# ReLU and mean over rows: input tiles of 8 rows in six buffers in place of 16 rows in three

## The chip, the cores and the metric

The kernel runs on one core of a Trainium2 chip. The metric is the device time of one execution in microseconds (us); lower is better. The time before is 164.88 us, the median of three runs (164.74 to 164.88).

## The reference

```python
batch, seq, dim = 32, 512, 1024
x = np.random.randn(batch, seq, dim).astype(np.float32)

relu_x = np.maximum(x, 0)
return np.mean(relu_x, axis=-1).astype(np.float32)
```

The input has 32 x 512 = 16,384 rows of 1,024 float32 values, 67.1 MB. For each row the kernel clips at zero and takes the mean: 16,384 results, 64 KB.

## The kernel before

The 16,384 rows are laid over 128 partitions, J = 128 consecutive rows on each (512 KB of contiguous input a partition). A tile `xt` holds NB = 16 rows of every partition: 128 partitions x 64 KB, 8.4 MB, and BUFS = 3 such buffers exist. The program is written out in full; there is no loop on the chip.

**Loads.** All loads are issued by SP (SyncE), in program order. Seven full tiles come with one transfer each (L79). A load waits until its buffer has been computed. The eighth tile comes in pieces: `row_pieces` halves what is left of the tile, so 8, 4, 2 and 1 rows (L86), and the last row comes as a half and two quarters (`col_pieces`, L90). That makes 14 loads.

**Compute.** `rows` (L62) gives even rows to ACT (ScalarE, L15) and odd rows to DVE (VectorE, L20). Each clips one row of 1,024 values in place and sums it into one column of `sum_a` or `sum_v`; in the trace each such call shows as two instructions, the work and the reading of the accumulator.

**Scaling.** `finish(lo, hi)` multiplies the sums by 1/1024 into `res`, odd columns on DVE (L73), even columns on ACT (L74). It runs twice: `finish(0, j0)` for all columns of the full tiles, placed ahead of the first piece of the last tile, and `finish(j0, j0 + lo)` behind the pieces but the last.

**End.** The last two rows are cut between ACT and DVE and put together by three small DVE instructions (L106, L111, L116), and one store of 64 KB (L120) writes `res`.

DMA transfers run on sixteen DMA engines. Each partition's share of a load is one contiguous run, so each engine gets eight data packets and one semaphore packet of a load; a load counts as landed when all sixteen semaphore packets have arrived. The trace has a record of each packet and each semaphore update.

Of the kernel before, what the change touches and what calls it, by code (L numbers as in the profile page):

```python
# [1 line left out]

# [4 lines left out]

F32 = mybir.dt.float32
ALU = mybir.AluOpType
RELU = mybir.ActivationFunctionType.Relu  # L10


def act_row(nc, src, acc):

    nc.scalar.activation(out=src, in_=src, func=RELU, accum_out=acc)  # L15


def dve_row(nc, src, acc):

    nc.vector.tensor_scalar(  # L20
        out=src, in0=src, scalar1=0.0, scalar2=None,
        op0=ALU.max, op1=ALU.add, accum_out=acc,
    )


@with_exitstack
def kernel(
    ctx: ExitStack,
    tc: tile.TileContext,
    x: bass.AP,  # L30
    out: bass.AP,
):
    nc = tc.nc
    P = nc.NUM_PARTITIONS
    xf = x.flatten_outer_dims()
    R, D = xf.shape
    assert R % P == 0
    J = R // P
    inv = 1.0 / D
    xr = xf.rearrange("(p j) d -> p j d", p=P, j=J)  # L40
    outr = out.flatten().rearrange("(p j) -> p j", p=P, j=J)

    NB = 16
    BUFS = 3
    full = J // NB - 1

    row_pieces = []
    left = NB
    while left > 1:
        row_pieces.append(left // 2)  # L50
        left -= left // 2
    col_pieces = [D // 2, D // 4, D // 4]

    in_pool = ctx.enter_context(tc.tile_pool(name="in", bufs=BUFS))
    res_pool = ctx.enter_context(tc.tile_pool(name="res", bufs=1))
    sum_a = res_pool.tile([P, J], F32)
    sum_v = res_pool.tile([P, J], F32)
    res = res_pool.tile([P, J], F32)
    part_a = res_pool.tile([P, 2], F32)
    part_v = res_pool.tile([P, 4], F32)  # L60

    def rows(xt, lo, n, j0):  # L62

        for k in range(lo, lo + n):
            j = j0 + k
            if j % 2:
                dve_row(nc, xt[:, k, :], sum_v[:, j:j + 1])
            else:
                act_row(nc, xt[:, k, :], sum_a[:, j:j + 1])

    def finish(lo, hi):

        nc.vector.tensor_scalar_mul(out=res[:, lo + 1:hi:2], in0=sum_v[:, lo + 1:hi:2], scalar1=inv)  # L73
        nc.scalar.mul(out=res[:, lo:hi:2], in_=sum_a[:, lo:hi:2], mul=inv)  # L74

    for t in range(full):
        j0 = t * NB
        xt = in_pool.tile([P, NB, D], F32, name="xt")
        nc.sync.dma_start(out=xt, in_=xr[:, j0:j0 + NB, :])  # L79
        rows(xt, 0, NB, j0)  # L80

    j0 = full * NB
    xt = in_pool.tile([P, NB, D], F32, name="xt")
    lo = 0
    for n in row_pieces:
        nc.sync.dma_start(out=xt[:, lo:lo + n, :], in_=xr[:, j0 + lo:j0 + lo + n, :])  # L86
        lo += n
    c = 0
    for w in col_pieces:
        nc.sync.dma_start(out=xt[:, lo, c:c + w], in_=xr[:, j0 + lo, c:c + w])  # L90
        c += w

    finish(0, j0)
    lo = 0
    for n in row_pieces[:-1]:
        rows(xt, lo, n, j0)
        lo += n
    finish(j0, j0 + lo)


    last = xt[:, NB - 1, :]
    act_row(nc, xt[:, lo, :D // 2], part_a[:, 0:1])
    dve_row(nc, xt[:, lo, D // 2:], part_v[:, 0:1])
    act_row(nc, last[:, :D // 4], part_a[:, 1:2])
    dve_row(nc, last[:, D // 4:D // 2], part_v[:, 1:2])
    nc.vector.tensor_scalar(  # L106
        out=res[:, J - 2:J - 1], in0=part_a[:, 0:1], scalar1=part_v[:, 0:1], scalar2=inv,
        op0=ALU.add, op1=ALU.mult,
    )
    dve_row(nc, last[:, D // 2:3 * D // 4], part_v[:, 2:3])  # L110
    nc.vector.tensor_scalar(  # L111
        out=part_v[:, 1:2], in0=part_v[:, 1:2], scalar1=part_a[:, 1:2], scalar2=part_v[:, 2:3],
        op0=ALU.add, op1=ALU.add,
    )
    dve_row(nc, last[:, 3 * D // 4:], part_v[:, 3:4])
    nc.vector.tensor_scalar(  # L116
        out=res[:, J - 1:J], in0=part_v[:, 3:4], scalar1=part_v[:, 1:2], scalar2=inv,
        op0=ALU.add, op1=ALU.mult,
    )
    nc.sync.dma_start(out=outr, in_=res)  # L120


# [1 line left out]
_INS = ['x']  # L124
_OUTS = [((32, 512), 'float32')]


# [23 lines left out]
```

## Time and profile before

| | |
|---|---|
| median of three runs | 164.88 us |
| the profiled execution | 164.88 us |
| its span in the profile | 163.1 us |
| DVE busy | 75.4 us (46%) |
| ACT busy | 69.4 us (43%) |
| DMA, load and store queue | 96.0% of 16 engines' span |
| bytes moved, mean rate | 67.19 MB, 412 GB/s |
| loads from HBM, stores | 14, 1 |

The span is what the profiler shows of the program on the core; the profiled execution's own time is longer by what lies around it. Busy shares are means over the whole span. "A <- B" behind an instruction names what ended the idle time ahead of it. SPq is the queue from which SP issues transfers, and its lines tell what an issue waited for. A line number is that of the kernel's source, so all rows on DVE stand under L20 and all rows on ACT under L15.

### The profile page before, as it was taken

To read this page: it belongs to the slowest core of one execution; us is meant where nothing else is said; L and a number is where in the kernel's file an instruction comes from. 1 tells how busy PE (TensorE), PEld (TensorE's weight loads), DVE (VectorE), ACT (ScalarE), POOL (GpSimd) and SP (SyncE) were. 2 spreads that over 40 slices of the span, in tenths; PEclk is the share of its full clock that TensorE was granted. 3 is DMA by queue.
4 is the path that set the end of the run, shared out by engine and by line. 5 is a ranking of instruction groups with operands and counts; after the bars stand their busy time and mean duration, and the time that the engine had idled before them with its cause. 6 is when DMAs were issued, how large, how long until landed. Compare 5 with 4: busy or idle time off the path is not lost.

```text
span 163.1 us, 351 instructions
## 1 busy us (share of the span) xinstructions
DVE 75.4 (46%) x139; ACT 69.4 (43%) x133; POOL 0.2 (0%) x4
## 2 busy tenths in 40 slices
DVE  0000039900596008940099202990059700799993
ACT  3000039700594008920099002980059500797890
POOL 0000000000000000000000000000000000000000
DMA  7979989989998998997997998998998897999970
GB/s 257 482 321 482 482 354 450 514 354 418 514 418 354 514 418 354 514 482 305 498 484 340 466 498 354 434 514 370 402 514 386 386 514 338 434 442 394 409 298 16
DMA packets 2162, 67.19 MB, mean 412 GB/s; under 512 B 240, under 2 KB 624, under 8 KB 880
## 3 DMA queue, kind: packets, MB, share of 16 engines
q1 hardware_dynamic: 2160, 67.18, 96.0%
q14 instruction: 2, 0.02, 0.0%
HBM read 67.11 MB, written 0.07 MB: 412 GB/s over the span
## 4 chain that ended last, share of the span: by engine, by line
DMA 83%; DVE 14%; SPq 1%; issue 0%; DVEq 0%
DMA xt<-in_x_dram 83%; DVE xt L20 13%; SPq L86 0%; SPq L79 0%; DVE part_v L111 0%; DVE res L116 0%; DVE res L106 0%; DVE res L73 0%; DVEq L20 0%; DVEq L111 0%; DVEq L106 0%
## 5 line engine op out<-in xcount | busy, mean ns | idle before, releaser
L20 DVE TENSOR_SCALAR_CACHE_REDUCE xt<-xt 128x1024 f32<-128x1024 f32 (+1 forms) x67 | 74.4, 1172 | 84.9 <-DMA xt<-in_x_dram 84.8
L15 ACT ACTIVATE xt<-xt 128x1024 f32<-128x1024 f32 (+1 forms) x65 | 66.7, 1027 | 88.9 <-DMA xt<-in_x_dram 88.9
L15 ACT ACTIVATION_READ_ACCUMULATOR xt<-xt 128x1 f32 x65 | 12.1, 187 | 0.0
L20 DVE DVE_READ_ACCUMULATOR xt<-xt 128x1 f32 x67 | 5.6, 83 | 0.0
L15 ACT ACT_TABLE_LOAD x1 | 1.3, 1283 | 0.7 <-PEq L135 0.7
L74 ACT ACTIVATE res<-sum_a 128x56 f32<-128x56 f32 (+1 forms) x2 | 0.5, 232 | 0.1
L73 DVE TENSOR_SCALAR res<-sum_v 128x56 f32<-128x56 f32 (+1 forms) x2 | 0.4, 184 | 0.1
L111 DVE TENSOR_SCALAR part_v<-part_v,part_a 128x1 f32<-128x1 f32 x1 | 0.3, 273 | 0.1
L106 DVE TENSOR_SCALAR res<-part_a,part_v 128x1 f32<-128x1 f32 x1 | 0.2, 214 | 0.1
L116 DVE TENSOR_SCALAR res<-part_v 128x1 f32<-128x1 f32 x1 | 0.2, 214 | 0.0
L135 POOL MEMSET const-uint8-127<- 128x1 uint8 x1 | 0.1, 102 | 0.0
L135 POOL MEMSET const-bfloat16-1.0<- 128x1 bf16 x1 | 0.1, 101 | 0.0
L135 POOL MEMSET const-float32-0.0<- 128x1 f32 x1 | 0.1, 98 | 0.2 <-issue 0.2
L135 POOL MEMSET const-float32-1.0<- 128x1 f32 x1 | 0.1, 98 | 0.0
## 6 DMA issues: line engine op xcount, KB each, us to landing
xt<-in_x_dram SPq DMA_DIRECT2D x1, 4096.0 KB, 39.0
xt<-in_x_dram SPq DMA_DIRECT2D x1, 2048.0 KB, 43.5
xt<-in_x_dram SPq DMA_DIRECT2D x1, 1024.0 KB, 45.5
xt<-in_x_dram SPq DMA_DIRECT2D x1, 512.0 KB, 46.3
xt<-in_x_dram SPq DMA_DIRECT2D x1, 256.0 KB, 46.5
xt<-in_x_dram SPq DMA_DIRECT2D x2, 128.0 KB, 42.7
xt<-in_x_dram SPq DMA_DIRECT2D x7, 48.9
out_dram<-res SPq DMA_DIRECT2D x1, 64.0 KB, 1.6
```

The lines of the kernel that those rows point to most:

```text
L15: nc.scalar.activation(out=src, in_=src, func=RELU, accum_out=acc)
L20: nc.vector.tensor_scalar(out=src, in0=src, scalar1=0.0, scalar2=None, op0=ALU.max, op1=ALU.add, accum_out=acc,)
L73: nc.vector.tensor_scalar_mul(out=res[:, lo + 1:hi:2], in0=sum_v[:, lo + 1:hi:2], scalar1=inv)
L74: nc.scalar.mul(out=res[:, lo:hi:2], in_=sum_a[:, lo:hi:2], mul=inv)
L106: nc.vector.tensor_scalar(out=res[:, J - 2:J - 1], in0=part_a[:, 0:1], scalar1=part_v[:, 0:1], scalar2=inv, op0=ALU.add, op1=ALU.mult,)
L111: nc.vector.tensor_scalar(out=part_v[:, 1:2], in0=part_v[:, 1:2], scalar1=part_a[:, 1:2], scalar2=part_v[:, 2:3], op0=ALU.add, op1=ALU.add,)
L116: nc.vector.tensor_scalar(out=res[:, J - 1:J], in0=part_v[:, 3:4], scalar1=part_v[:, 1:2], scalar2=inv, op0=ALU.add, op1=ALU.mult,)
L135: nc = _bacc.Bacc("TRN2", target_bir_lowering=False, num_devices=1)
```

## The change

The tile holds 8 rows and there are six buffers. All else follows from these two constants: `full` goes from 7 to 15 tiles, a load of a full tile brings 32 KB a partition, and the last tile's `row_pieces` are 4, 2 and 1 rows, with the last row cut as before. `finish(0, j0)` covers 120 columns in place of 112, and `finish(j0, j0 + lo)` 6 in place of 14. Buffer memory is the same, 192 KB a partition.

```diff
-    NB = 16
-    BUFS = 3
+    NB = 8
+    BUFS = 6
     full = J // NB - 1
```

## The prediction

> **What bounds the kernel now.** I read the page first, for engines against DMA, then the chain that ended last, then the timeline where a tile lands, then the waits of the queue that issues the loads.
>
> ```profile
> span 163.1 us, 351 instructions
> DVE 75.4 (46%) x139; ACT 69.4 (43%) x133; POOL 0.2 (0%) x4
> DMA packets 2162, 67.19 MB, mean 412 GB/s; under 512 B 240, under 2 KB 624, under 8 KB 880
> q1 hardware_dynamic: 2160, 67.18, 96.0%
> DMA 83%; DVE 14%; SPq 1%; issue 0%; DVEq 0%
> ```
>
> Both compute engines work less than half of the span; the sixteen DMA engines work 96% of it, and the chain is 83% load. The packet counts say how loads are cut: 2162 - 880 = 1282 packets are of 8 KB or more, and these are 7 x 128 of 64 KB, 3 x 128 of 32, 16 and 8 KB and 2 instruction packets. So a descriptor of 64 KB runs as one packet.
>
> ```profile
> 120.25 1.06 ACT L15 ACTIVATE xt<-xt 128x1024 f32<-128x1024 f32 x1 [10.93 <-DMA xt<-in_x_dram]
> ...
> 139.60 1.06 ACT L15 ACTIVATE xt<-xt 128x1024 f32<-128x1024 f32 x1 [10.94 <-DMA xt<-in_x_dram]
> ...
> 149.29 1.06 ACT L15 ACTIVATE xt<-xt 128x1024 f32<-128x1024 f32 x1 [0.97 <-DMA xt<-in_x_dram]
> ...
> 154.12 1.22 DVE L20 TENSOR_SCALAR_CACHE_REDUCE xt<-xt 128x1024 f32<-128x1024 f32 x1 [0.16 <-DMA xt<-in_x_dram]
> ...
> 156.62 1.06 ACT L15 ACTIVATE xt<-xt 128x1024 f32<-128x1024 f32 x1 [0.30 <-DMA xt<-in_x_dram]
> ```
>
> The first number is when the engine starts on fresh rows: a 16-row tile takes 19.35 us to arrive, the 8-row piece 9.69, the 4-row piece 4.83, the 2-row piece 2.50. Compute waits for each. DVE, which starts at the same moments, no longer waits after 156.62: from there it runs its own row work to 160.6, then the store.
>
> ```profile
> SPq L79 <- DVE xt L20: 87.4, 4, 30.4
> SPq L86 <- DVE xt L20: 19.2, 1, 19.2
> SPq L90 <- DMA xt<-in_x_dram: 7.2, 1, 7.2
> ```
>
> SP, which issues the loads, waits for free buffers, but this starves nothing. A load is issued when a tile is computed, about 9.3 us after it landed, and two tiles are still queued: 2 x 19.35 - 9.3 = 29 us of cover. The third line shows a second limit: the last load was issued at 120.16, when tile 5 landed (120.14), the load eight places ahead of it.
>
> **The base.** The profiled execution took 164.88 us, span 163.1 and 1.78 around it; that is also the median of the three runs. So a change of the span is added to 164.88 directly. About 0.2% (0.33 us) is what a measurement of this kernel can tell from no change.
>
> **What does not change in bytes or rows.** 64 rows for each engine, the same three part rows, the same three DVE combinations at the end. Buffers: 6 x 32 KB = 3 x 64 KB. The last seven arrivals before were pieces of 8, 4, 2, 1 rows and three parts; now a full tile of 8 rows, then 4, 2, 1 and three parts: the same sizes in the same order.
>
> **Cost of the halved loads (on the path).** Loads go from 14 (7 + 4 + 3) to 21 (15 + 3 + 3), seven more, all ahead of the last eight rows. The semaphore records of the landings are finer than engine starts. Undisturbed 16-row tiles landed 19.354 us apart; 8 rows took 149.208 - 139.501 = 9.707, then 4 rows 4.894, 2 rows 2.492, 1 row 1.293. Two 8-row loads are 2 x 9.707 = 19.414, so halving one tile costs 0.060. Seven tiles: 0.42 us. From the smaller pieces the same constant comes out larger: 2 x 4.894 - 9.707 = 0.081, 2 x 2.492 - 4.894 = 0.090, 2 x 1.293 - 2.492 = 0.094. Seven times 0.094 is 0.66, the upper end.
>
> The packet records say why. On most engines a 64 KB packet follows its predecessor after 2.414 us and a 32 KB packet after 1.209, so two small ones cost 0.004 more; with 8 packets an engine and load, 56 more packets, that is 0.22, and seven more semaphore packets of about 6 ns 0.04: 0.27 us, the lower end. On the engines that end last the figures are about 2.418 and 1.213, so 0.008 a pair: 0.45 + 0.04 = 0.49 if it held all along. The last engine sets the landing, so I take the landings' 0.42, between 0.27 and 0.66. No hole hides it: consecutive packets on an engine leave no gap.
>
> Two rules of the Trainium skill bear on this step and say different things. The page "DMA: Bandwidth & Descriptors", section "Why small descriptors are slow (HBM only)", gives some 3 cycles of a bus per packet; with the 850 MHz that the page's specifications give, an estimate is 3.5 ns x 56 = 0.2 us, which would make 165.1. Its section on the anatomy of one DMA gives about 2.0 us fixed per DMA (there for the software path), which speaks against the change: paid seven times in line it would make 14 us and 179 us. The landings contradict the second as a cost of throughput, since a further load in a full queue cost 0.06 to 0.09.
>
> **Issue.** SP issues 22 transfers for 15, each 0.33 to 0.44 us, off the path as long as engines have queued work. Cover after: a tile of 8 rows is computed about 4.7 us after landing (4 x 1.14 + 0.1), and five are queued: 5 x 9.71 - 4.7 = 44 us. The pieces, which the eight-places limit holds back: the 4-row load goes when tile 9 is computed (105 us), the last quarter when tile 12 lands, near 130, for data due near 159.6. Nothing runs dry, so I take 0. But issuing disturbs: where SP issued six loads at 110.2 to 112.5, one 64 KB packet of nearly every engine took some 45 ns longer; at single issues about 10. Seven more issues cost 7 x 0.01 = 0.07, at most 7 x 0.045 = 0.3, or nothing if the engine that ends last is missed; I take nothing, since the 19.354 already holds one issue each.
>
> **First load.** The first packet of each engine took 2.72 to 3.49 us (mean 3.18) where later ones took 2.42: 0.76 us of start-up, once. The second packet shows none. If it is latency, 32 KB packets pay the same 0.76; if it grew with size, half is saved. Bounds 0 and -0.76; I take 0, because it is gone at once, which a cost by bytes would not be. The first tile will land near 13.5 us, earlier; no one gains from it.
>
> **Instruction fetch.** Two 8 KB instruction packets at 85.0 and 87.4 us lengthened one interval: tile 3 to tile 4 took 19.569, 0.21 over the rest, and the later landings stayed late. After, the same instructions are reached some ten us sooner; I take the same 0.21, with bounds 0 and twice that (-0.21 to +0.21).
>
> **Tail.** `finish(0, j0)` scales 60 columns an engine where it scaled 56 and moves behind the last full tile, so between the 8 rows and the 4-row piece. On DVE the 8 rows end at 153.97 on the clock of before; the scaling (0.20 us) starts about 0.03 later. At the second `finish` the next row started 0.08 after it (157.88, 157.96), so here the row starts near 154.1 to 154.2, where it started at 154.12. Two rows take 2.37, ending at 156.5 to 156.57, before the 2-row piece at 156.59. Covered; if not, 0.2 at most. ACT ends its 8 rows at 153.56 and has the room. From the 2-row piece on, the work is unchanged: `finish` on 3 columns for 7 is a few ns. Cost 0.
>
> **Sum.** 164.88 + 0.42 = 165.30, span about 163.5.
>
> **The rivals.** (A) The price is that of the undisturbed engines, or the instruction fetch falls on an engine with room: 164.88 + 0.27 = 165.15, or 164.88 + 0.42 - 0.21 = 165.09. For: 13 of 16 engines run at 1.209 us for 32 KB; engines end up to 1.17 us apart, so there is room on most. Against: the engines with the fetch land last. Within 0.2%. (B) The other side: start-up shrinks with the packet. If all 0.76 goes: 164.88 + 0.42 - 0.76 = 164.54. It decides once more than 0.75 of it is gone (0.42 - 0.75 = -0.33). Against: only one packet an engine shows it. (C) Issues disturb at the rate seen at 111 us: 165.30 + 0.3 = 165.60, or the scaling on DVE runs into the 2-row piece: 165.50. Against: single issues at 51 and 71 us show some 10 ns. That the change does nothing is excluded as a rival: the 32 KB pieces run as 32 KB packets.
>
> **How the numbers follow.** Forecast (165.30 to 165.54) 0.60, all slower by over 0.2% (above 165.21); A 0.24, within 0.2%; B 0.06, faster; C 0.10, slower. So faster 0.06, same 0.24, slower 0.70. The range goes from 164.95, under A by about the 0.14 that three runs scatter, to 165.70, the end of C with that of the forecast inside; outside lie B and the ends of A and C.
>
> **What would show it.** Right: 3,168 packets on the load queue (21 x 128 data, 22 x 16 semaphores, 128 of the store); tiles landing every 9.71 us from about 13.5; the 2-row piece near 157.0; DVE waiting a little (0.02 to 0.1) ahead of it; an unchanged 4.0 us from there to the store's issue; a median issue to landing near 6 x 9.71 - 4.7 = 53.6 us. Wrong: landings 9.68 apart (A), a first landing before 13.2 (B), intervals over 9.75 or DVE late at the 2-row piece (C), or any stretch of the middle with DMA share under 0.95, which would mean that the queue ran dry.

## The result and the profile after

The changed kernel took 165.46 us (median of four runs, 165.26 to 165.79) against 164.86 us for the kernel before in the same comparison: ratio 1.0040, 95% interval 1.0022 to 1.0058. On a second occasion, with more runs, it was 165.42 (11 runs) against 165.08 (29 runs): ratio 1.0023, interval 1.0014 to 1.0032. It is slower by 0.3 to 0.6 us. The profiled execution is the slowest of the first four, 165.79 us, with a span of 164.0.

The page of the changed kernel, the lines that answer to those of before:

```profile
span 164.0 us, 373 instructions
DVE 76.0 (46%) x139; ACT 70.1 (43%) x133; POOL 0.2 (0%) x4
DMA packets 3170, 67.19 MB, mean 410 GB/s; under 512 B 352, under 2 KB 736, under 8 KB 992
q1 hardware_dynamic: 3168, 67.18, 96.1%
DVE 35%; another core or an unknown queue 30%; DMA 30%; SPq 1%; issue 1%; DVEq 0%
xt<-in_x_dram SPq DMA_DIRECT2D x15, 4096.0 KB, 53.8
```

The compute engines do the same instructions, the DMA engines are as busy as before (96.1%), and there are 1,008 more packets for the same bytes: 896 of data and 112 of semaphores. The chain looks quite different, 30% DMA for 83%, and that is a trap: with six buffers the program that followed the chain could not name what ended many of the waits ("an unknown queue") and put the computing of tiles into it. The engines' own waits show that nothing has moved to DVE:

```profile
ACT xt L15 <- DMA xt<-in_x_dram: 89.0, 17, 11.4
DVE xt L20 <- DMA xt<-in_x_dram: 85.1, 15, 13.4
SPq L79 <- DVE xt L20: 89.5, 9, 14.0
SPq L90 <- DMA xt<-in_x_dram: 22.3, 3, 9.4
```

Before, the two engines' lines were:

```profile
ACT xt L15 <- DMA xt<-in_x_dram: 88.9, 10, 21.2
DVE xt L20 <- DMA xt<-in_x_dram: 84.8, 9, 23.2
```

DVE waited 85.1 us for loads, before 84.8. The timeline at the end of the stream gives the arrivals:

```profile
140.45 1.06 ACT L15 ACTIVATE xt<-xt 128x1024 f32<-128x1024 f32 x1 [5.45 <-DMA xt<-in_x_dram]
...
150.16 1.06 ACT L15 ACTIVATE xt<-xt 128x1024 f32<-128x1024 f32 x1 [5.44 <-DMA xt<-in_x_dram]
...
154.88 0.20 DVE L73 TENSOR_SCALAR res<-sum_v 128x60 f32<-128x60 f32 x1
155.07 1.22 DVE L20 TENSOR_SCALAR_CACHE_REDUCE xt<-xt 128x1024 f32<-128x1024 f32 x1
...
157.47 1.06 ACT L15 ACTIVATE xt<-xt 128x1024 f32<-128x1024 f32 x1 [0.24 <-DMA xt<-in_x_dram]
157.47 1.22 DVE L20 TENSOR_SCALAR_CACHE_REDUCE xt<-xt 128x1024 f32<-128x1024 f32 x1
...
161.52 0.35 SPq L120 DMA_DIRECT2D out_dram<-res  x1
```

A tile of 8 rows takes 9.71 us. The scaling stands where the prediction put it, at 154.88, and the 4-row piece (landed at 154.953) starts on DVE at 155.07, 0.03 behind ACT (155.04); two rows later DVE is back in step, at 157.47 like ACT. From there to the store's issue it is 4.05 us, as before, where the 2-row piece started at 156.62 and the store was this line:

```profile
160.67 0.35 SPq L120 DMA_DIRECT2D out_dram<-res  x1
```

So the whole difference lies ahead of the 2-row piece: it landed at 157.446, before at 156.594, 0.852 later.

The semaphore records of the trace split these 0.852 us. The usual interval between two landings is called undisturbed, and what other intervals have over it excess. Before: start-up 3.856 (first landing 23.210 less one undisturbed tile of 19.354), seven tiles 135.478, pieces of 8, 4 and 2 rows 17.093, and 0.167 by which some intervals exceeded the undisturbed one. After: start-up 3.699, fifteen tiles at an undisturbed 9.712 = 145.680, pieces 7.389, and 0.678 of excess. So the loads themselves cost +0.495 (145.680 - 135.478 - 9.707), the start gave back 0.157, and 0.511 is excess: 0.331 in the interval with the instruction fetch (before 0.215), and 0.318 in three early intervals of 9.797, 9.921 and 9.736, in which many 32 KB packets took 1.24 to 1.36 us in place of 1.213.

### The profile page after: what moved, and what is told of

It reads as the page before. It is cut to its first block, busy times and chain, and to the rows that moved or that the text cites. A ratio compares the mean times of both kernels' runs of the same rounds, so it can differ in the third digit from the quotient of the medians.

```text
span 164.0 us, 373 instructions
## 1 busy us (share of the span) xinstructions
DVE 76.0 (46%) x139; ACT 70.1 (43%) x133; POOL 0.2 (0%) x4
## 3 DMA queue, kind: packets, MB, share of 16 engines
q1 hardware_dynamic: 3168, 67.18, 96.1%
## 4 chain that ended last, share of the span: by engine, by line
DVE 35%; another core or an unknown queue 30%; DMA 30%; SPq 1%; issue 1%; DVEq 0%
DVE xt L20 34%; DMA xt<-in_x_dram 30%; SPq L79 1%; DVEq L20 0%; DVE res L73 0%; DVE part_v L111 0%; DVE res L106 0%; DVE res L116 0%; DVEq L111 0%; DVEq L106 0%
## 5 line engine op out<-in xcount | busy, mean ns | idle before, releaser
L20 DVE TENSOR_SCALAR_CACHE_REDUCE xt<-xt 128x1024 f32<-128x1024 f32 (+1 forms) x67 | 75.0, 1172 | 85.2 <-DMA xt<-in_x_dram 85.1
L74 ACT ACTIVATE res<-sum_a 128x60 f32<-128x60 f32 (+1 forms) x2 | 0.5, 232 | 0.1
## 6 DMA issues: line engine op xcount, KB each, us to landing
xt<-in_x_dram SPq DMA_DIRECT2D x15, 4096.0 KB, 53.8
```

Source lines behind the costliest of these rows:

```text
L20: nc.vector.tensor_scalar(out=src, in0=src, scalar1=0.0, scalar2=None, op0=ALU.max, op1=ALU.add, accum_out=acc,)
```

## The experiments

Two theories stood at the outset: L, that cutting the loads costs DMA-engine time; and S, that chance stretches (the 0.511) make the difference. A third, B, puts it on buffers, release order and interleaving. Each median below is against the kernel before run on the same chip beside it.

**The changed kernel again.** No edit.

> The changed kernel once more, beside the others. Theory L (the seven further loads cost DMA-engine time, 0.06 us each, plus stretches where packets run longer): 0.4 to 0.7 us over the kernel before. Theory S (the difference is mostly chance in where stretches of longer packets and the instruction fetch fall): between 0 and 0.9 us, and not the same from run to run.

165.42 us against 165.08: +0.34. This time the profile (165.35 us) has no early stretch: the first eight landings are 9.70 to 9.72 apart, and the only long interval is the one with the fetch, 9.900. The early stretch is chance and not part of the change; the undisturbed interval is again 9.712, so the loads cost the same +0.495 without it. S falls as the main cause.

**Two loads of 8 rows a tile, all else as before.**

```diff
-        nc.sync.dma_start(out=xt, in_=xr[:, j0:j0 + NB, :])
+        for h in range(0, NB, 8):
+            nc.sync.dma_start(out=xt[:, h:h + 8, :], in_=xr[:, j0 + h:j0 + h + 8, :])
```

> The kernel before (16 rows, three buffers), but each full tile fetched by two loads of 8 rows: 21 loads and 3,168 load-queue packets as in the changed kernel, buffers and scaling as before. Theory L: the same 0.4 to 0.7 us over the kernel before as the changed kernel. Rival B (buffers, order of release, the finer interleaving with compute make the difference): within 0.1 us of the kernel before.

165.47 us, ratio 1.0025 (1.0016 to 1.0034): +0.39 with the old buffers. B falls: the loads alone bring the whole difference.

**One load a tile, but packets of 32 KB.** A gap of 64 bytes (PAD = 16 values) halfway through each buffer keeps a partition's 64 KB from being one run.

```diff
-        xt = in_pool.tile([P, NB, D], F32, name="xt")
-        nc.sync.dma_start(out=xt, in_=xr[:, j0:j0 + NB, :])
+        xt = in_pool.tile([P, 2, 8 * D + PAD], F32, name="xt")
+        nc.sync.dma_start(
+            out=xt[:, :, :8 * D],
+            in_=xr[:, j0:j0 + NB, :].rearrange("p (a b) d -> p a (b d)", a=2, b=8),
+        )
...
```

> The kernel before with a gap of 64 bytes in the middle of each buffer, so that a full tile is still one load (14 loads) but in packets of 32 KB: 56 more data packets an engine, no further semaphore packets. If the price is by packet: 0.25 to 0.5 us over the kernel before, most of what the changed kernel pays. If it is by load: 0 to 0.1 us.

165.41 us, ratio 1.0025 (1.0015 to 1.0036): +0.33. The page of this kernel shows seven loads of 8 MB in twice as many packets:

```profile
q1 hardware_dynamic: 3056, 67.18, 95.7%
xt<-in_x_dram SPq DMA_DIRECT2D x7, 8192.0 KB, 49.7
```

3,056 packets are those of the changed kernel less 7 x 16 semaphore packets. Fourteen loads of small packets cost what twenty-one do: the price is by packet, and seven more loads as such cost nothing that these runs can tell (the three medians with 32 KB packets lie within 0.06 us, each known to some 0.17). Its profiled execution was a long one, 166.13, with two intervals of 20.138 and 19.792, the second with the fetch. Its other four are 19.378 to 19.445, mean 19.416: 0.06 over 19.354, and no further load is in it. Whether the gap in the buffer has a price of its own this kernel does not tell; the tiles of 24 rows below have no gap.

**Three buffers of 8 rows for six.** `BUFS = 6` became `BUFS = 3`.

> The changed kernel with three buffers of 8 rows in place of six: cover of the load queue 2 x 9.71 - 4.7 = 14.7 us in place of 44. Theory L: as the changed kernel, 0.4 to 0.7 us over the kernel before, since 14.7 us still suffices. If six loads issued at the start caused the longer packets between 10 and 32 us: about 0.3 us less than the changed kernel. If depth matters: more than 1 us over.

165.42 us, ratio 1.0024 (1.0014 to 1.0035). Issue to landing fell from 53.8 to 24.3 us, half the time queued, and nothing changed. Depth is worth nothing here. The early intervals are clean (9.692 to 9.722), but so were those of the changed kernel's second profile, which has six issues at the start; these issues alone do not lengthen packets.

**The two kernels with a quarter of the compute in all but the last eight rows.**

```diff
         for k in range(lo, lo + n):
             j = j0 + k
+            if j < J - NB2 and k % 8 not in (0, 7):
+                continue
```

NB2 is 8. The two kernels leave out the results of six of every eight rows; the sums are set to zero at the start.

> The kernel before with six of every eight rows left uncomputed in all but the last eight rows (all loads stay): each engine has a quarter of its row work there, so few instructions that the fetch of 8 KB of instructions in the middle should not be needed. If the fetch costs what its interval showed: about 0.2 us under the kernel before. If compute has a part in the stream's pace: more than 0.3 us under. Else the same within 0.1.

> The changed kernel with the same rows left uncomputed as in the light kernel of 16 rows. Packet theory: 0.25 to 0.45 us over that light kernel, as with the full compute. Rival (the packets are only longer beside compute, or the later instruction fetch makes the difference): within 0.1 us of it.

164.84 us with tiles of 16 rows, 0.25 under the kernel before (ratio 0.9985, 0.9976 to 0.9994), and 165.29 with tiles of 8 rows: 0.45 between them, as with full compute or a little more. So the price does not come from compute that runs beside the packets: with a quarter of it the difference is no smaller. Neither has an instruction packet within its stream. In the light 8-row kernel all fourteen intervals lie between 9.693 and 9.720, so there the long interval near 85 us is gone with the fetch. In the light 16-row kernel one interval of 19.621 remained, where packets near 65 us took 2.57 to 2.84 us, with no fetch. The 0.25 agree with the fetch's 0.2, but such stretches are of the same size, so this is likely and not shown.

**Tiles of 4 rows, twelve buffers.** `NB = 4`, `BUFS = 12`.

> The changed kernel with 4 rows a tile and twelve buffers: 36 loads, packets of 16 KB, 120 more data packets an engine than with 8 rows. At the 0.34 us that 56 packets cost, 6 ns each: 0.73 us over the changed kernel, 1.07 over the kernel before, about 166.1; between 0.5 and 1.0 over the changed kernel if 4 to 8.5 ns. If the price were fixed for any tile smaller than 64 KB a partition: no more than the changed kernel.

166.70 us, ratio 1.0098 (1.0082 to 1.0113): +1.28 over the changed kernel's 165.42, more than expected.

```profile
DMA packets 5330, 67.19 MB, mean 407 GB/s; under 512 B 592, under 2 KB 976, under 8 KB 1232
```

A dose of 120 more data packets an engine brings more time, so the price does not stop at one step. Loads grow in the same proportion here (15 more), so this run does not tell loads from packets. By the landings, undisturbed 4-row tiles are 4.894 apart: 2 x 4.894 - 9.712 = 0.076, fifteen times is 1.14. I had priced a packet from the measured 0.34 and so expected 0.73. But the start gave back 0.41 (first landing 8.233 - 4.894 = 3.34; the changed kernel's second profile had 3.75), which cancels this error. What is left of the miss lies in one interval, that with the fetch: 5.649, 0.755 too long where that profile had 0.19. The three terms make 1.30; the 2-row landings of the two profiles are 1.27 apart (158.279 and 157.007). Why that interval was so long stays open.

**The end of the kernel.** The 4 us between the 2-row piece and the store were the same in both kernels, and 1.4 us of them come after the last landing (159.185 to 160.60). This version of the kernel before moves the first half of the last row to ACT, scaled on the way, and lets ACT put the row together.

```diff
-    act_row(nc, last[:, :D // 4], part_a[:, 1:2])
-    dve_row(nc, last[:, D // 4:D // 2], part_v[:, 1:2])
+    nc.scalar.activation(out=last[:, :D // 2], in_=last[:, :D // 2], func=RELU, scale=inv, accum_out=part_a[:, 1:2])
...
+    nc.scalar.activation(out=part_b, in_=part_v[:, 2:3], func=RELU, scale=inv, bias=part_a[:, 1:2])
+    dve_row(nc, last[:, 3 * D // 4:], part_w)
+    nc.scalar.activation(out=res[:, J - 1:J], in_=part_w, func=RELU, scale=inv, bias=part_b)
```

> The kernel before (16 rows, three buffers) with another end: ACT takes the first half of the last row already scaled by 1/1024, DVE the last two quarters, and two small ACT instructions put the row together, in place of two quarters' work and two combining instructions on DVE. The last data lands at 159.19 and DVE ends its rows near 159.65 in place of 160.35; the result is ready near 159.95 in place of 160.60: 0.6 us under the kernel before, about 164.3, if compute after the last landing sets the end. If the store waits for something else: no gain.

164.51 us, ratio 0.9965 (0.9952 to 0.9978): 0.58 faster than the kernel before, and faster than both kernels of this case. In its timeline the last data had landed at 159.245:

```profile
159.30 0.41 DVE L20 TENSOR_SCALAR_CACHE_REDUCE xt<-xt 128x256 f32<-128x256 f32 x1
159.48 0.30 ACT L112 ACTIVATE part_b<-part_v,part_a 128x1 f32<-128x1 f32 x1
...
159.82 0.29 ACT L114 ACTIVATE res<-part_w,part_b 128x1 f32<-128x1 f32 x1
160.14 0.35 SPq L115 DMA_DIRECT2D out_dram<-res  x1
```

The store goes 0.53 earlier than before (160.67), although its last load landed 0.06 later.

**The same end on the changed kernel.**

> The changed kernel (8 rows, six buffers) with the new end of the last row. If packets and end add up: 0.58 us under the changed kernel's 165.42, so about 164.85, 0.2 us under the kernel before. If the smaller tiles leave the end a different shape: any other gain than 0.5 to 0.65.

164.85 us against 165.13 for the kernel before: 0.28 under it (ratio 0.9989, 0.9979 to 0.9999), and 0.57 less than the changed kernel's 165.42. Taken each against the kernel before beside it, the new end gave -0.58 and the smaller tiles +0.34, together -0.24. The two effects add up.

**Tiles of 24 rows in two buffers, with that end.** `NB = 24`, `BUFS = 2`, five tiles, and the last 8 rows in pieces as in the changed kernel.

> Tiles of 24 rows in two buffers (five of them), the last 8 rows in pieces of 4, 2, 1 rows and parts, and the new end. A partition's 96 KB go as two descriptors of 48 KB, so 128 data packets an engine where tiles of 16 rows have 112. Packet theory (some 8 ns each): 0.13 us over the 16-row kernel with the new end, about 164.6 to 164.65. If larger tiles or fewer loads (11 for 14) paid by themselves: under 164.5. If cover of one tile less its compute, 29 - 14 = 15 us, were too little: over 165.

173.49 us, ratio 1.0504 (1.0489 to 1.0518): over 165, but not for want of cover. The DMA share was 0.98 to 1.03 in every stretch from 10 to 150 us and the last part row landed at 159.787, but DVE was late:

```profile
149.97 1.22 DVE L20 TENSOR_SCALAR_CACHE_REDUCE xt<-xt 128x1024 f32<-128x1024 f32 x1 [15.31 <-DMA xt<-in_x_dram]
...
164.79 0.19 DVE L76 TENSOR_SCALAR res<-sum_v 128x60 f32<-128x60 f32 x1
164.90 1.21 DVE L20 TENSOR_SCALAR_CACHE_REDUCE xt<-xt 128x1024 f32<-128x1024 f32 x1
```

The last full tile lands all at once at 149.83, and its twelve rows on DVE, 1.14 us each, last until 163.7, while the 8 rows behind it needed only 10 us to arrive and then queued behind them. I had counted queue and packets and not the work behind the last big landing. Its landings still add a point: undisturbed tiles were 29.044 and 29.071 apart in packets of 48 KB, where one and a half tiles of 16 rows make 29.031. So with fewer loads and more packets for the same rows, and no gap in the buffer, they came some 0.03 later. Two intervals are few, but this too speaks for packets and against loads.

## Why the prediction held, point by point

- **What bounds the kernel: right.** Compute ahead of the last eight rows can be cut to a quarter, or buffers halved, with a change of 0.25 us at most; more packets for the same bytes move the time.
- **The price of the cut: right in size, wrong in name.** The prediction took 0.060 us "per load" from the landings, 0.42 in all, with 0.27 to 0.66 as bounds. Measured undisturbed, two 8-row loads cost 2 x 9.712 - 19.354 = 0.070, or 0.49. The kernel with padded buffers shows that it goes with packets: 0.495 / 56 = 8.8 ns each, the few semaphore packets (9 ns each) counted in. By packet size, 8 rows took 9.677 us (64 KB), 9.686 (48 KB), 9.712 (32 KB), 9.788 (16 KB); an engine moves them in 4, 5.3, 8 and 16 packets, so each further packet cost 7 to 10 ns. The 4 ns read on undisturbed engines were too low, and so was rival A. The prediction put the difference on the engines that end last; the semaphores show that it is paid on all sixteen. From the first of a landing's sixteen semaphores to the last, each comes 9.712 to 9.714 us after the one of its place in the landing before, in the changed kernel's second profile, and 19.347 to 19.357 in the kernel before (medians over the tiles). Eight packets at the usual spacing of 1.209 make 9.672 and do not fill these 9.712; what fills the rest stays open. The Trainium skill ("DMA: Bandwidth & Descriptors", "Why small descriptors are slow (HBM only)") gives a cost by packet, and so the right kind; the estimate of 3.5 ns from it is under half of what these landings show.
- **Issue: right at 0 in the likeliest case.** The longer packets at 111 us are no chance: in all three profiles with 64 KB packets (before, light, new end), 13 to 16 packets that started where six issues stand together (111.3 to 112.3 us, in the light kernel 104 to 105.2) took 2.44 to 2.48 us in place of 2.42. But the tiles in flight landed 19.348 to 19.363 apart, as undisturbed, so it cost nothing that the landings show. With 32 KB packets the mark is absent: 1.219 at most beside the six issues of the padded kernel, and 1.225 at most between 5 and 85 us in the second profile of the changed kernel, with seven single issues in that time. Rival C falls with that. The stretch between 10 and 32 us in the first profile is another matter: the second has the same issues and not the stretch.
- **First load: 0 was a little off.** (The first packets' mean is 3.17 by the records, the start-up in them 0.75.) By the landings, start-up was 3.86, 3.74 and 3.69 us in three profiles of 16-row loads, 3.64 to 3.75 in six of 8-row loads, 3.34 with 4 rows. So 8 rows save some 0.07, less than the scatter, and rival B's 0.76 is excluded: 0.42 was the most seen, with packets of a quarter.
- **Instruction fetch: same place, other size.** Taken as 0.21 both times; in full-compute profiles with 8-row loads its interval was 0.19 to 0.55 too long, so it adds scatter, and no run tells its sign.
- **Tail: right.** The scaling left DVE 0.03 us behind ACT, which was made good before the 2-row piece; 4.05 us from there to the store in both.
- **The marks.** 3,168 packets, tiles every 9.71 and 53.8 us from issue to landing came as written; the 2-row landing, 157.0 by the forecast, was 157.45 in the first profile (early stretch and fetch) and 157.01 in the second. 165.30 was forecast; 165.46 and 165.42 were measured. As differences, 0.42 was forecast and 0.60 and 0.34 were measured. That these lie so near is in part luck: the loads cost 0.495, the start gave some of it back and the stretches added some, where the prediction had the start unchanged and no stretches.

## What to carry to other kernels

Where the load queue never runs dry, count packets, not loads and not buffers: here 56 more packets an engine cost 0.3 to 0.5 us of 165, seven more loads and half the depth cost nothing that could be told. A finer tile pays only for compute that waits behind the last big landing; check that this work fits into the arrival of what follows, or a coarse last tile costs far more (8.4 us over the kernel before) than its packets save. With the stream fixed, the work after the last landing is where a kernel like this still gives: moving half a row and the final sums to the idle engine gave 0.58 us.

## What the runs showed of the hardware that was not expected

- Packets of one size run longer in stretches that differ between executions of the same kernel: in one profile of the changed kernel many 32 KB packets between 10 and 32 us took 1.24 to 1.36 us for 1.213, in the next none there. The cause stays open.
- In all ten profiles with full compute there are two 8 KB instruction packets in mid-stream (309 ns each when alone), and the tile interval that holds them was 0.19 to 0.75 us too long (with three buffers they fell in two intervals, and only that of the second was long). The kernels with a quarter of the compute had none in the stream. Intervals as long occur without them too (20.138 in the padded kernel, 19.621 in the light one), so the packets are the likely cause and not the shown one.
- With six loads issued within some 2.3 us, the 64 KB packets then on the engines took some 45 ns longer in three profiles of three, and 32 KB packets no longer in the one profile that has both; the landings show no cost of it.
- Semaphores and issues of seven more loads left no mark, with 21 loads or 14.
